# One kind of seven-product unit, with two weight sums kept in DRAM and two added where used: 66 units instead of 60

## The chip, the core and the metric

The kernel runs on one core of one Trainium2 chip. The core has a matrix engine (TensorE, PE in the profile; its weight loads are shown as PEld), a vector engine (VectorE, DVE), a scalar engine (ScalarE, ACT), a general engine (GpSimd, POOL) and a queue engine (SyncE, SP) that issues most of the transfers. TensorE writes into PSUM; the other operands live in SBUF, on 128 partitions, and the weights come from DRAM. The metric is the device time of one execution in microseconds (us); lower is better.

## The reference

A trunk of two pre-norm residual layers over 256 tokens of width 2048, in float32. Layer 0 mixes tokens by neighbourhood attention, layer 1 by a gated short convolution. After each comes a gated MLP of inner width 5632 with a depthwise convolution.

```python
def conv_glu_ffn(x, w_up, conv_w, conv_b, w_down):
    h = dwconv_centered(x @ w_up, conv_w) + conv_b
    g, u = jnp.split(h, 2, axis=-1)
    return (jax.nn.silu(g) * u) @ w_down

def reference(x, ...):
    h = x
    for i in range(DEPTH):
        a = rms_norm(h, mix_norm[i])
        ...
        h = h + mixed
        h = h + conv_glu_ffn(rms_norm(h, ffn_norm[i]), ...)
    return rms_norm(h, final_norm)
```

## The kernel before

**Precision.** Each float32 operand is split into a high part (a cast to the matmul type, ACT, L171 or L294) and a low part (what the cast left over, DVE, L172 or L295). A product is then three matmuls into one PSUM tile: high by high, high by low, low by high.

**Two kinds of stage.** A `Phase` computes one 128-column tile of a projection after another (query/key, up projection, short-conv input); its weight tile is the stationary operand, and its evacuations on ACT and DVE (convolution, gate, split into the next stage's activation tiles) lie beside the following matmuls. `Values` does the attention's values. A `Tokens` stage computes an output projection: `wo` after attention, two halves of the down projection in each layer (`down[layer, half]`, 22 tiles of input width each), and `wscout` after the short convolution (16 tiles). In a `Tokens` stage the activations are the stationary operand and the weights move, 512 columns at a time.

**Units.** A `Tokens` stage works on two groups `g` of 1024 output columns. In each it goes over pairs of input tiles; such a pair, with two halves of the tokens and two halves of the columns, is a unit: a two-by-two block product. A plain unit (P) does it with eight products, 24 matmuls. A seven-product unit does it with seven, 21 matmuls, after a scheme that needs four sums of blocks on either side. On the activation side these are the forms (`make_forms`, GpSimd and split, made in the stage before). On the weight side they are `t1` to `t4`, and there are two kinds of unit for them:

- S ("sums"): `left` and `right` blocks (512 KB each) are loaded, DVE adds all four sums where the unit is used (L180, L181, L183, L184, four adds of 128x512), and `w22`, `t1`/`t3` and `t4`/`t2` are split.
- D ("kept"): the four sums were made earlier and kept in DRAM. The unit loads `left` (512 KB), the block `w22` (256 KB, half a buffer) and two tiles of kept sums (512 KB each) and splits all four.

**Making sums ahead.** `make` (L189) handles half of a D unit: two loads of 256 KB into activation tiles that happen to be free (L199), four adds of 128x256 (L206 to L209) due four chunks later, two stores of 256 KB from ACT's queue (L214) due seven chunks later. `plan_jobs` lists these half jobs and `take` deals them out over the attention, up and short-conv stages that come before their use: `QK_JOBS`, `V_JOBS`, `UP_JOBS`, `SC_JOBS`.

**Order.** The plans (`S_FIRST`, `S_SECOND`, `S_OUT`, `S_ATT`) write out by hand, for each group, which unit is of which kind and in which order they run, and after how many items the combination of the unit's four extra PSUM tiles into `h` (`combine`, eight DVE operations) is due. There are 60 seven-product units: 12 in each of the four down projections, 8 in `wscout`, 4 in `wo`; 38 of them D and 22 S, of 120 units in all. What is loaded and split runs ahead of the matmuls by chunks (`prep_to`, `AHEAD` = 4): six `raw` buffers for what is loaded (`RAWS`), six each for high and low parts (`hi`, `lo`). A framework places the instructions on each engine's queue in an order of its own, close to that of the program; the engines then run in order.

**PSUM and SBUF.** The forms of the even tiles' three other blocks lie in six slots of the tags `sf`, `vv` and `qk`; the fourth goes over a quarter of the activation tile that no seven-product unit reads (`place`). There are 22 activation tiles.

Of the kernel before, what the change touches and what calls it, by code (L numbers as in the profile page):

```python
# [22 lines left out]
P = 128  # L23
# [22 lines left out]
def plan(text, due):  # L46


    words = text.split()
    return (tuple(int(x[1:]) for x in words), {int(x[1:]): x[0] for x in words if x[0] != "P"}, due)  # L50


S_FIRST = (plan("P0 D1 P2 S3 D4 P5 D6 S7 P8 D9 P10", 3), plan("P0 P2 D1 S3 D4 P5 D6 S7 P8 P10 D9", 6))
S_SECOND = (plan("P0 P2 D1 S3 D4 P5 D6 S7 D8 P9 P10", 1), plan("P0 P2 P5 D1 S3 D4 S7 D6 D8 P9 P10", 1))
S_OUT = (plan("P0 D1 S2 P3 D4 D5 P6 P7", 1), plan("P0 P3 D1 S2 D4 D5 P6 P7", 1))
QK_JOBS, V_JOBS, UP_JOBS, SC_JOBS = (0, 4, 4, 2), (2, 2, 2, 0), (10, 10, 12, 8), 20
S_ATT = (plan("P0 P1 P2 S6 P3 S7 P4 P5", 1),) * 2

# [19 lines left out]
def trunk(ctx, tc, xT, par, bias, wqk, wv, wo, wsc, wscout, wup, wdown, out):  # L78
# [49 lines left out]
    def prep_to(n):  # L128
        while len(prepped) < min(n, len(chunks)):
# [4 lines left out]
            if kind == "make":  # L134
                make(src, w)
                prepped.append(())
                continue
# [6 lines left out]
            if kind == "kept":  # L144
                newest["SP"] = nc.sync.dma_start(out=raw, in_=src().rearrange("p h n -> p (h n)"))
            else:
                newest["SP"] = nc.sync.dma_start(out=raw[:, :4 * w].rearrange("p (f c) -> p f c", f=4),
                                                 in_=src.rearrange("f p c -> p f c"))
            r = raw[:, :4 * w].rearrange("p (f k c) -> p f k c", f=4, c=P)
            if kind != "sums":  # L150
                prepped.append(parts(r) + (raw,))
            else:
                prepped.append(sums(prepped[-1][2].rearrange("p (f k c) -> p f k c", f=4, c=P), r))
# [21 lines left out]
    def sums(l, r):  # L175

        t13 = wp.tile([P, CH * P], F32, name="raw", tag="raw", bufs=RAWS)
        v13 = t13.rearrange("p (k f c) -> p f k c", f=4, c=P)
        add = nc.vector.tensor_add
        add(out=v13[:, :, 0, :], in0=l[:, :, 0, :], in1=r[:, :, 0, :])  # L180
        add(out=v13[:, :, 1, :], in0=r[:, :, 1, :], in1=r[:, :, 0, :])  # L181
        w22 = parts(r[:, :, 1:2, :])
        add(out=r[:, :, 1, :], in0=v13[:, :, 0, :], in1=r[:, :, 1, :])  # L183
        add(out=r[:, :, 0, :], in0=r[:, :, 1, :], in1=l[:, :, 1, :])  # L184
        return w22, parts(t13), parts(r)

    kept, newest = {}, {}

    def make(job, half):  # L189

        w, g, i = job
        if half == 0:
            kept[id(w), g, i] = dp.tile([P, 2, 2, 4 * P], F32, name=f"kept{len(kept)}")
        dst = kept[id(w), g, i]
        tiles = [act_tile().bitcast(F32) for _ in range(2)]
        for n, x in enumerate(tiles):
            f = 8 * g + 4 * n + 2 * half
            with tc.issue_after(newest["SP"].ins):
                nc.sync.dma_start(out=x.rearrange("p (f n) -> p f n", f=2),  # L199
                                  in_=w[f:f + 2, :, 2 * i * P:(2 * i + 2) * P].rearrange("f p n -> p f n"))  # L200
        l, r = (x.rearrange("p (f k c) -> p k f c", f=2, k=2) for x in tiles)

        def adds():
            add = nc.vector.tensor_add
            with tc.issue_after(newest["DVE"].ins):
                add(out=l[:, 0], in0=l[:, 0], in1=r[:, 0])  # L206
                add(out=r[:, 0], in0=r[:, 1], in1=r[:, 0])
                add(out=r[:, 1], in0=l[:, 0], in1=r[:, 1])
                add(out=l[:, 1], in0=r[:, 1], in1=l[:, 1])  # L209

        def store():
            for n, x in enumerate(tiles):
                with tc.issue_after(newest["ACT"].ins):
                    nc.scalar.dma_start(out=dst[:, n, half], in_=x)  # L214
        stores.append((len(prepped) + 4, adds))
        stores.append((len(prepped) + 7, store))
# [3 lines left out]
    def plan_jobs(w, plans):  # L220
        jobs.extend(((w, g, i), half) for g, (order, kinds, _) in enumerate(plans) for i in order if kinds.get(i) == "D"
                    for half in range(2))
# [5 lines left out]
    class Phase:  # L228
# [3 lines left out]
        def __init__(self, w, fts, nk, src, evac, intro=0, step=CH, jobs=()):  # L232
# [9 lines left out]
            for n, (two, ks) in enumerate(order):  # L242
# [5 lines left out]
                while made < min(len(jobs), max(0, -(-len(jobs) * (n + 1 - lo) // (hi - lo)))):  # L248
                    chunks.append((*jobs[made], "make"))
# [130 lines left out]
    class Tokens:  # L380
# [4 lines left out]
        def __init__(self, w, nk, src, evac, plan, forms, halves=0):  # L385
# [4 lines left out]
            for g, (order, kinds, _) in enumerate(plan):  # L390
                for i in order:
# [10 lines left out]
                    if kinds.get(i) == "S":  # L402
                        chunks.append((right, 2 * P, "sums"))
                        items.append((self, g, c + 1, k, k, k + 2))
                        ends.append(c + 2)
                    elif i in kinds:
                        chunks.append((right[:, :, P:], P, "cols"))
                        chunks.extend((lambda j=j, key=(id(w), g, i): kept[key][:, j], 2 * P, "kept") for j in range(2))
                        items.append((self, g, c + 1, k, k, k + 2))
                        ends.append(c + 4)  # L410
# [50 lines left out]
        def seven(self, g, c, k0):  # L461
# [8 lines left out]
            if sset[i] == "S":  # L470
                w22, (t1, t3), (t4, t2) = prepped[c][0], *([(y, j) for j in range(2)] for y in prepped[c][1:])
            else:
                w22, (t1, t4), (t3, t2) = prepped[c], *([(y, j) for j in range(2)] for y in prepped[c + 1:c + 3])
            s1, s2, s4, s3 = self.forms[i]
            raw = lambda k, t: tuple(self.src[k0 + k][:, j + t * P:j + (t + 1) * P] for j in (0, S))
            for ps, x, (w, j) in ((a, raw(0, 0), (left, 0)), ("11", raw(1, 0), (left, 1)), ("12", s4, (w22, 0)),
                                  (e, s1, t1), *((("21", raw(1, 1), t4),) * (sset[i] == "D")), (f, s3, t3), (b, s2, t2),
                                  *((("21", raw(1, 1), t4),) * (sset[i] == "S"))):
# [26 lines left out]
    form_at = [3]  # L505

    def make_forms(xe, xo, place):

        v = tp.tile([P, 4, P], F32, name="s", tag="s")
# [5 lines left out]
        if isinstance(place, tuple):  # L515
# [4 lines left out]
        n = form_at[0] = (form_at[0] + 1) % 6  # L520
        y = tp.tile([P, 6 * P], F32R, name="sf", tag=("sf", "vv", "qk")[n % 3])
        hi, lo = y[:, :3 * P], y[:, 3 * P:]
        split_into(hi, lo, v[:, :3].rearrange("p f c -> p (f c)"))
        spare = place[:, P:2 * P], place[:, 3 * P:]
        split_into(*spare, v[:, 3])
        return [(hi[:, j * P:(j + 1) * P], lo[:, j * P:(j + 1) * P]) for j in (0, 1)] + [
            spare, (hi[:, 2 * P:], lo[:, 2 * P:])]
# [116 lines left out]
    class Values:  # L644


        def __init__(self, g, src, jobs=()):
            self.g, self.src = g, src
            for k0 in range(0, KT, 2):
# [3 lines left out]
                if k0 in (4, 8)[:len(jobs)]:  # L653
                    chunks.append((*jobs[k0 // 8], "make"))
# [31 lines left out]
    def sc_evac(f, ps):  # L686
# [11 lines left out]
        else:  # L698
# [3 lines left out]
            if j % 2 == 0:  # L702
                sc_of["even"] = t
            elif j // 2 in S_OUT[0][1]:
                yforms[j // 2] = make_forms(sc_of["even"], t, yT[j - 1])
# [4 lines left out]
    def up_evac(layer, act, forms, sset):  # L710
        def evac(f, ps):
# [11 lines left out]
            else:  # L723
# [5 lines left out]
                elif j % HALF // 2 in sset:  # L729
                    forms[j % HALF // 2] = make_forms(glu["even"], c, act[j % HALF - 1])  # L730
# [247 lines left out]
```

## Time and profile before

| what | us |
|---|---|
| median of 3 runs | 2204.2 (2204.12 to 2206.07) |
| the profiled execution | 2203.89 |
| its span | 2202.1 |

The profile's page gives each engine's busy time with its share of the span and its number of instructions; then the span in 40 slices (PEclk is the TensorE clock that was granted, in tenths of full speed); then the chain of work that ended last, followed back from the last instruction. The views of the trace name a group or an instruction by its line in the kernel, its engine, its operation and its tiles (out <- in); a number in brackets behind an instruction of the timeline is how long the engine was idle before it, and who ended that. The matmuls are pipelined: the listed duration of one is longer than the step to the next.

| queue | packets | MB | share of 16 engines |
|---|---|---|---|
| SP's loads (q1) | 265360 | 488.07 | 68.3% |
| ACT's stores (q10) | 23264 | 40.49 | 4.9% |

### The profile page before, as it was taken

The page shows a single profiled execution, that of the slowest core. Times are in us where ns is not written, and L with a number is a line of the kernel's source. Part 1 is how long each engine was busy: PE and PEld are TensorE (multiplying, and loading weights), DVE is VectorE, ACT ScalarE, POOL GpSimd, SP SyncE. Part 2 cuts the span into 40 slices and gives each one's busy share as a digit, 9 for nine tenths or more (in the row PEclk, how much of TensorE's full clock was granted, in tenths as well). Part 3 has the DMA queues.
Part 4 walks back from the last instruction along what each step waited for, and adds up shares of the span by engine and source line. Part 5 has one row for each costly group of instructions (what it writes and reads, how often), then busy time and mean ns, then how long its engine had stood idle before and what let it go on. Part 6 is the DMA issues. An engine that isn't in the chain of part 4 may idle for free.

```text
span 2202.1 us, 33145 instructions
## 1 busy us (share of the span) xinstructions
PE 2184.6 (99%) x11728; PEld 1891.3 (86%) x11728; DVE 1835.8 (83%) x2960; ACT 1288.7 (59%) x1967; POOL 90.5 (4%) x143
## 2 busy tenths in 40 slices
PE   9999999999999999999999999999999999999997
PEld 8888888888888888888788888888888888888886
DVE  8788778888888788888897787898888887888888
ACT  7554556665655556566664445566656565666565
POOL 1001000000000000000000000000000000001000
PEclk9999999999999999999999999999999999999999
DMA  8787746777657777767798886787776786776585
GB/s 293 242 275 254 248 149 210 251 247 243 218 182 253 273 239 247 252 210 239 231 338 262 285 277 200 241 272 245 249 250 199 231 273 231 248 244 225 173 267 173
DMA packets 288790, 530.67 MB, mean 241 GB/s; under 512 B 19568, under 2 KB 187632, under 8 KB 288624
## 3 DMA queue, kind: packets, MB, share of 16 engines
q1 hardware_dynamic: 265360, 488.07, 68.3%
q10 hardware_dynamic: 23264, 40.49, 4.9%
q8 instruction: 92, 1.51, 0.3%
q14 instruction: 74, 0.61, 0.1%
HBM read 486.54 MB, written 41.94 MB: 240 GB/s over the span
## 4 chain that ended last, share of the span: by engine, by line
PE 88%; DVE 5%; DMA 5%; issue 1%; ACT 1%; SPq 0%; DVEq 0%; ACTq 0%
PE mm L262 40%; PE mm L270 21%; PE mm L458 6%; PE mm L459 6%; PE mm L457 6%; DMA act<-in_wdown 2%; DVE lo L172 2%; PE mu L458 2%; PE mu L459 2%; PE mu L457 2%; DMA raw<-in_wdown 1%; PE mm L665 1%; PE mm L667 1%; PE mm L666 1%; ACT hi L171 1%
## 5 line engine op out<-in xcount | busy, mean ns | idle before, releaser
L171 ACT CAST hi<-raw 128x1024 fp32r<-128x1024 f32 (+1 forms) x912 | 903.7, 1012 | 344.0 <-PE mm L459 91.7
L172 DVE TENSOR_TENSOR lo<-raw,hi 128x1024 fp32r<-128x1024 f32 (+1 forms) x852 | 1012.0, 1210 | 104.0 <-ACT hi L171 67.0
L262 PE MATMUL mm<-a,hi 128*128 128x512 f32 x4096 | 961.6, 391 | 0.5 <-DVE a L303 0.5
L262 PEld LDWEIGHTS mm<-a,hi 128*128 128x128 f32 x4096 | 759.2, 188 | 152.8 <-DVE a L303 1.6
L270 PEld LDWEIGHTS mm<-a,lo 128*128 128x128 f32 x4096 | 512.9, 191 | 14.3 <-DVE lo L172 2.4
L270 PE MATMUL mm<-a,lo 128*128 128x256 f32 x4096 | 518.6, 283 | 2.0 <-DVE lo L172 2.0
L457 PE MATMUL mm<-hi,act 128*128 128x512 f32 x656 | 255.7, 390 | 0.2 <-DVE h L350 0.2
L459 PE MATMUL mm<-hi,act 128*128 128x512 f32 x656 | 255.5, 390 | 0.0
L458 PE MATMUL mm<-lo,act 128*128 128x512 f32 x600 | 233.9, 390 | 0.6 <-DVE lo L172 0.5
L329 ACT ACTIVATE conv<-pad,pt 128x256 f32<-128x256 f32 x176 | 105.7, 601 | 205.6 <-DVE pad L321 203.8
L331 DVE SCALAR_TENSOR_TENSOR conv<-pad,pt,conv 128x256 f32<-128x256 f32 x384 | 183.8, 480 | 21.9 <-ACT conv L329 16.9
L315 ACT COPY corr<-mm 128x256 f32<-128x256 f32 x256 | 91.4, 370 | 163.1 <-PE mm L270 135.4
L457 PEld LDWEIGHTS mm<-hi,act 128*128 128x128 f32 x656 | 123.1, 188 | 25.9 <-issue 0.6
L459 PEld LDWEIGHTS mm<-hi,act 128*128 128x128 f32 x656 | 123.1, 188 | 25.4
L458 PEld LDWEIGHTS mm<-lo,act 128*128 128x128 f32 x600 | 112.7, 188 | 24.9 <-DVE lo L172 1.9
L316 DVE TENSOR_TENSOR corr<-mm,corr 128x256 f32<-128x256 f32 x256 | 106.7, 417 | 5.3 <-ACT corr L315 5.1
L206 DVE TENSOR_TENSOR act<-act 128x256 f32<-128x256 f32 x76 | 32.7, 431 | 75.7 <-DMA act<-in_wdown 59.6
L295 DVE TENSOR_TENSOR act<-conv,act 128x256 fp32r<-128x256 f32 x88 | 37.4, 425 | 60.6 <-ACT act L294 60.6
L321 DVE TENSOR_TENSOR pad<-corr,rstd 128x256 f32<-128x256 f32 x176 | 73.8, 419 | 0.2
L458 PE MATMUL mu<-lo,sf 128*128 128x512 f32 x168 | 65.9, 392 | 1.8 <-DVE lo L172 1.8
L459 PE MATMUL mu<-hi,sf 128*128 128x512 f32 x168 | 65.4, 389 | 0.0
L457 PE MATMUL mu<-hi,sf 128*128 128x512 f32 x168 | 65.4, 389 | 0.0
(158 smaller groups left out, 1540.3 us busy)
## 6 DMA issues: line engine op xcount, KB each, us to landing
raw<-in_wup SPq DMA_DIRECT2D x352, 512.0 KB, 5.2
raw<-in_wdown SPq DMA_DIRECT2D x144, 512.0 KB, 5.5
raw<-in_wsc SPq DMA_DIRECT2D x96, 512.0 KB, 5.6
kept<-act ACTq DMA_DIRECT2D x152, 256.0 KB, 4.1
raw<-kept SPq DMA_DIRECT2D x76, 512.0 KB, 4.9
act<-in_wdown SPq DMA_DIRECT2D x128, 256.0 KB, 5.9
raw<-in_wqk SPq DMA_DIRECT2D x56, 512.0 KB, 5.3
raw<-in_wv SPq DMA_DIRECT2D x32, 512.0 KB, 4.7
```

The costliest lines, as they stand in the source:

```text
L171: newest["ACT"] = nc.scalar.copy(out=hv, in_=r)
L172: newest["DVE"] = nc.vector.tensor_sub(out=lv, in0=r, in1=hv.bitcast(F32))
L262: nc.tensor.matmul(self.ps[ft], lhsT=prepped[i][0][:, o:o + P], rhs=self.src[k], start=k == 0, stop=False)
L270: nc.tensor.matmul(self.ps[ft][:, S:], lhsT=prepped[i][1][:, o:o + P], rhs=self.src[k][:, :S], start=False, stop=k == self.nk - 1)
L315: nc.scalar.copy(out=corr, in_=ps[:, S:])
L316: nc.vector.tensor_add(out=corr, in0=ps[:, :S], in1=corr)
L321: nc.vector.tensor_mul(out=dst, in0=both(ps), in1=rstd)
L329: nc.scalar.activation(c, x[:, 1:S + 1], AF.Identity, scale=w[1], bias=b)
L331: nc.vector.scalar_tensor_tensor(out=c, in0=x[:, tap:tap + S], scalar=w[tap], in1=c, op0=ALU.mult, op1=ALU.add)
L457: nc.tensor.matmul(ps, lhsT=xh, rhs=wh, start=start, stop=False)
L458: nc.tensor.matmul(ps, lhsT=xh, rhs=wl, start=False, stop=False)
L459: nc.tensor.matmul(ps, lhsT=xl, rhs=wh, start=False, stop=stop)
```

## The change

S and D units are replaced by one kind, H. Of the four weight sums `t1` and `t3` are kept in DRAM, as one tile of 512 KB, and `t2` and `t4` are added where the unit is used: `pair_of_sums` writes `t2 = t1 + w22` over the loaded `w22` in its own raw buffer, and `t4 = t2 +` a block of `left` into the half of that buffer that was empty; the buffer is then split as a whole. A job now handles a whole unit: three loads of 256 KB, two adds of 128x512, two stores of 256 KB.

```diff
+S_FIRST = (plan("P0 H1 H3 P2 H4 H5 P8 H6 H7 H9 P10", 3), plan("P0 P2 H1 H3 P8 H4 H5 H6 P10 H7 H9", 6))
+S_SECOND = plan("P0 P2 H1 H3 H4 P9 H5 H6 H7 H8 P10", 0)
+S_MLP = {(0, 0): S_FIRST, (0, 1): (S_SECOND, plan("P0 P2 P5 H1 H3 H4 P9 H6 H7 H8 P10", 0)),
+         (1, 0): S_FIRST, (1, 1): (plan("P0 P2 H1 H3 H4 P9 H6 H7 H8 P5 P10", 1), plan("P0 P2 H1 H3 P5 H4 H6 H7 P8 P9 P10", 0))}
+S_OUT = (plan("P0 H1 H2 P3 H4 H5 H7 P6", 0), plan("P0 P3 H1 H2 H4 H5 H7 P6", 0))
+S_ATT = (plan("P0 P1 P2 H6 P3 H7 P4 P5", 1),) * 2
+QK_JOBS, V_JOBS, UP_JOBS, SC_JOBS = (0, 4, 4, 0), (2, 3, 2, 0), (9, 8, 11, 8), 16
...
             if kind == "kept":
-                newest["SP"] = nc.sync.dma_start(out=raw, in_=src().rearrange("p h n -> p (h n)"))
...
+                newest["SP"] = nc.sync.dma_start(out=raw, in_=src())
+                t13 = parts(raw)
+                prepped.append((t13, parts(pair_of_sums(raw, prepped[-1][2], prepped[-2][2]))))
+                continue
...
+    def pair_of_sums(t13, w22, left):
+
+        l = left.rearrange("p (f k c) -> p k f c", f=4, c=P)
+        t2, t4 = w22[:, :4 * P], w22[:, 4 * P:].rearrange("p (f c) -> p f c", f=4)
+        nc.vector.tensor_add(out=t2, in0=t13[:, :4 * P], in1=t2)
+        nc.vector.tensor_add(out=t4, in0=t2.rearrange("p (f c) -> p f c", f=4), in1=l[:, 1])
+        return w22
...
-    def make(job, half):
...
+    def make(w, g, i):
+
+        kept[id(w), g, i] = dst = dp.tile([P, 8 * P], F32, name=f"kept{len(kept)}")
+        tiles = [act_tile().bitcast(F32) for _ in range(3)]
+        for x, f, k in zip(tiles, (0, 4, 4), (0, 0, 1)):
+            f, k = 8 * g + f, 2 * i + k
             with tc.issue_after(newest["SP"].ins):
...
+                nc.sync.dma_start(out=x.rearrange("p (f c) -> p f c", f=4),
+                                  in_=w[f:f + 4, :, k * P:(k + 1) * P].rearrange("f p c -> p f c"))
+        l, r, t = tiles
 
         def adds():
...
+                nc.vector.tensor_add(out=l, in0=l, in1=r)
+                nc.vector.tensor_add(out=t, in0=t, in1=r)
```

The units by stage become 4 in `wo`, 14 and 13 in layer 0's down projections, 10 in `wscout`, 14 and 11 in layer 1's. The two halves of the MLP now have plans for each layer (`S_MLP`), and the combination's due times change with them. In `seven` the product with `w22` and the four with sums keep their order, with the one that needs `t4` last. The forms follow: where a unit is of seven products in only one of the two groups, the fourth form can no longer lie over the activation tile, and gets a block of its own; a seventh form of a half is put into what the larger slots leave over.

```diff
+    form_at, left_over = [], []
+
+    def form_slots(blocks):
+
+        if not form_at:
+            return [left_over.pop() for _ in range(3)]
+        tag = next(x for x in form_at if blocks == 3 or x != "sf")
+        form_at.remove(tag)
+        y = tp.tile([P, (6 if tag == "sf" else 8) * P], F32R, name="sf", tag=tag)
+        if tag != "sf" and blocks == 3:
+            left_over.append(y[:, 6 * P:])
+        return y
```

The jobs of the value stage stand behind its second, fourth and sixth chunk instead of the third and fifth.

More of the change, by code (lines that the diff above doesn't have):

```diff
@@ L173, in split_parts @@
         return hi, lo
[L175 to L185, printed above, removed]
@@ L220, in plan_jobs @@
     def plan_jobs(w, plans):
-        jobs.extend(((w, g, i), half) for g, (order, kinds, _) in enumerate(plans) for i in order if kinds.get(i) == "D"
-                    for half in range(2))
+        jobs.extend((w, g, i) for g, (order, sset, _) in enumerate(plans) for i in order if i in sset)
     def take(n):
@@ L704, in sc_evac, with up_evac @@
             elif j // 2 in S_OUT[0][1]:
-                yforms[j // 2] = make_forms(sc_of["even"], t, yT[j - 1])
+                yforms[j // 2] = make_forms(sc_of["even"], t, in_both(S_OUT, j // 2) and yT[j - 1], not yforms)
     glu = {}
-    def up_evac(layer, act, forms, sset):
+    def up_evac(layer, act, forms, plans):
         def evac(f, ps):
```

116 lines of the change are left out of this document (47 added, 69 removed).

## The prediction

> **What bounds the kernel now.** I read the page first, its busy shares and the chain that ended last, then TensorE's own waits, the windows of the stretches in which two-by-two units run, and in these the VectorE's timeline.
>
> ```profile
> PE 2184.6 (99%) x11728; PEld 1891.3 (86%) x11728; DVE 1835.8 (83%) x2960; ACT 1288.7 (59%) x1967; POOL 90.5 (4%) x143
> PEclk9999999999999999999999999999999999999999
> PE 88%; DVE 5%; DMA 5%; issue 1%; ACT 1%; SPq 0%; DVEq 0%; ACTq 0%
> ...
> PE bc L781 <- DVE conv L779: 3.7, 2, 3.2
> PE mm L270 <- DVE lo L172: 2.0, 2, 1.1
> PE mu L458 <- DVE lo L172: 1.8, 4, 0.7
> PE st L111 <- DVE inv L740: 1.1, 1, 1.1
> ...
> PE mm L458 <- DVE lo L172: 0.5, 1, 0.5
> ```
>
> TensorE is at work in 99% of the span, at full granted clock, and 88% of the chain is its own matmuls. Its waits are small: 3.7 us belong to the closing norm, and what is left for faster feeding is 2.0 + 1.8 + 0.5 = 4.3 us, all of it waits for VectorE's low part of a weight block (L172). So a matmul less is time less, as long as VectorE keeps pace; VectorE, at 83%, is the engine that could stop it. By stretch, the columns being us, busy PE, PEld, DVE, ACT, POOL, clock, DMA share, GB/s:
>
> ```profile
> 306.00:394.00 88.00, 88.00 (x408) 73.36 (x408) 71.67 (x90) 51.36 (x72) 4.84 (x8) 1.00 0.60 196
> 641.84:753.39 111.55, 111.55 (x495) 92.35 (x493) 92.52 (x107) 66.91 (x74) 0.00 (x0) 1.00 0.77 251
> 997.85:1108.90 111.05, 109.78 (x489) 89.56 (x488) 96.88 (x116) 69.75 (x88) 0.00 (x0) 1.00 0.75 250
> 1113.86:1385.10 271.24, 269.25 (x1553) 238.07 (x1552) 211.24 (x375) 137.51 (x201) 9.61 (x16) 1.00 0.81 264
> 1385.10:1468.00 82.90, 82.90 (x376) 68.67 (x375) 73.63 (x91) 52.08 (x67) 0.00 (x0) 1.00 0.79 261
> 1716.90:1828.44 111.54, 111.54 (x494) 92.35 (x493) 92.42 (x107) 67.10 (x74) 0.00 (x0) 1.00 0.77 251
> 2072.91:2190.00 117.09, 115.79 (x522) 94.72 (x520) 98.86 (x125) 70.10 (x92) 0.00 (x0) 1.00 0.66 217
> ```
>
> In order: `wo`; first and second down projection of layer 0; the short-conv input projection; its output projection; first and second down projection of layer 1, the last with part of the end. TensorE fills all but 1.3 us of each down projection and all of the output projection.
>
> **What the change removes: 18 matmuls.** A plain unit (P) issues 8 products of 3 matmuls, a seven-product unit 21. The first down projection of layer 0 has 12 seven-product and 10 plain units, 12 x 21 + 10 x 24 = 492 matmuls in 111.55 us: 0.227 us each. (A matmul's listed duration, 390 ns, is its latency; they overlap.) Six more units make 6 x 3 x 0.227 = 4.08 us less on the engine that sets the end. By the plans: +2 in each first down projection, +1 and -1 in the second ones, +2 in the output projection, none in `wo`.
>
> **VectorE's price of a unit**, by starts in its timeline of the first down projection:
>
> ```profile
> 698.65 2.35 DVE L172 TENSOR_TENSOR lo<-raw,hi 128x1024 fp32r<-128x1024 f32 x2
> 700.91 0.68 DVE L499 TENSOR_TENSOR h<-h,mu 128x512 f32<-128x512 f32 x1
> ...
> 703.92 0.68 DVE L172 TENSOR_TENSOR hi<-raw,hi 128x512 fp32r<-128x512 f32 x1
> 704.52 2.35 DVE L172 TENSOR_TENSOR lo<-raw,hi 128x1024 fp32r<-128x1024 f32 x2
> ```
>
> Two low parts of 1024 take 2.26 us from start to start, 1.13 each; the five adds of 512 from 700.91 to 703.92 take 0.60 each, and so does a low part of 512. Hence P: 2 x 1.13 = 2.26. A D unit (sums all kept in DRAM): 3 x 1.13 + 0.60 = 3.99. An S unit (all sums made where used): 3.99 + 4 x 0.60 = 6.39. The new H unit, with two adds where used: 3.99 + 1.20 = 5.19. TensorE gives a seven-product unit 21 x 0.227 = 4.77 us and a P unit 5.45. So D ran ahead of TensorE, H falls 0.4 us behind it each time, and only P units win that back. By stretch:
> - first down projections: 8 D + 4 S + 10 P = 80.1 becomes 14 H + 8 P = 90.7. VectorE 92.5 + 10.7 = 103.2 us in 111.55 - 1.36 = 110.2: 94%.
> - second, layer 0: 13 H + 9 P = 87.8, +7.7: 104.6 of 110.4, 95%.
> - output projection: 6 D + 2 S + 8 P = 54.8 becomes 10 H + 6 P = 65.5. 73.6 + 10.7 = 84.3 of 81.5 us: 103%.
> - second, layer 1: 11 H + 11 P = 82.0, +1.9: 100.8 of 117.8, 86%, and its last unit goes.
> - `wo`: 4 S become 4 H, -4.8 us: no risk.
>
> The output projection's excess must come from the lead with which VectorE enters:
>
> ```profile
> 1383.37 0.69 DVE L181 TENSOR_TENSOR raw<-raw 128x512 f32<-128x512 f32 x1
> ...
> 1385.36 0.40 PE L457 MATMUL mm<-hi,act 128*128 128x512 f32 x1
> ```
>
> When TensorE starts on unit 0, VectorE has for 2 us been at the sums of unit 2, which TensorE needs 5.45 + 4.77 us later: a lead of some 10 us.
>
> **The wait that H adds.** ACT may cut the second pair of sums into its high part only after the second add, and VectorE then waits for ACT. The S unit has the same chain, and its cost is to be seen (VectorE, ACT, TensorE):
>
> ```profile
> 1087.89 0.68 DVE L184 TENSOR_TENSOR raw<-raw 128x512 f32<-128x512 f32 x1
> 1089.77 2.36 DVE L172 TENSOR_TENSOR lo<-raw,hi 128x1024 fp32r<-128x1024 f32 x2 [1.19 <-ACT hi L171]
> ...
> 1088.69 4.49 ACT L171 CAST hi<-raw 128x1024 fp32r<-128x1024 f32 x5 [2.01 <-DVE raw L184]
> ...
> 1091.05 0.50 PE L458 MATMUL mu<-lo,sf 128*128 128x512 f32 x1 [0.75 <-DVE lo L172]
> ...
> 676.16 0.69 DVE L184 TENSOR_TENSOR raw<-raw 128x512 f32<-128x512 f32 x1
> 676.77 5.91 DVE L172 TENSOR_TENSOR lo<-raw,hi 128x1024 fp32r<-128x1024 f32 x5
> ```
>
> At 1087.89 the last sum leaves VectorE idle for 1.19 us and TensorE for 0.75; at 676.16 another low part was ready and it cost nothing. Queued behind a waiting low part are VectorE's later low parts and the combine, and TensorE waits for these. So H's wait lies between 0 and 1.19 us; I take 0.6, the middle, as both rows are of the same operation. Then the demand is 103.2 + 14 x 0.6 = 111.6 of 110.2 in the first down projections, 104.6 + 7.8 = 112.4 of 110.4 in the second of layer 0, 84.3 + 6.0 = 90.3 of 81.5 in the output projection: short by 1.4, 2.0 and 8.8 us, each under the lead of 10. The last leaves 1.2 us, and late in a run of H units the lead is no longer whole. I put 2.0 us of new TensorE waits there (bounds 0 and 5).
>
> **Sums, loads and stores ahead.** 76 half jobs of four adds of 256 become 66 jobs of two of 512.
>
> ```profile
> 1267.02 0.43 DVE L206 TENSOR_TENSOR act<-act 128x256 f32<-128x256 f32 x1 [3.90 <-DMA act<-in_wdown]
> ...
> 1269.84 0.42 DVE L209 TENSOR_TENSOR act<-act 128x256 f32<-128x256 f32 x1
> 1270.17 0.42 DVE L206 TENSOR_TENSOR act<-act 128x256 f32<-128x256 f32 x1
> ...
> 1271.78 0.62 PE L270 MATMUL mm<-a,lo 128*128 128x256 f32 x3 [0.86 <-DVE lo L172]
> ...
> raw<-in_wdown SPq DMA_DIRECT2D x144, 512.0 KB, 5.5
> kept<-act ACTq DMA_DIRECT2D x152, 256.0 KB, 4.1
> raw<-kept SPq DMA_DIRECT2D x76, 512.0 KB, 4.9
> ...
> raw<-in_wdown SPq DMA_DIRECT2D x32, 256.0 KB, 3.9
> ```
>
> By starts an add of 256 is 0.33 us, so 76 x 4 x 0.33 = 100 us become 66 x 2 x 0.60 = 79. These lie beside the up and short-conv projections, where TensorE sets the pace, and are worth nothing by themselves; they can ease the 0.86 us and its like. Stores fall from 152 to 132 on ACT's queue. SP issues 3 loads a job instead of 2 a half job, 198 for 152, and one read back a unit for two. Bytes of a unit: 1 MB of job traffic each way and 1.75 MB at use for D; for H 0.75 in, 0.5 out, 1.25 at use. S and P units have no job and draw 1 MB. In all 38 x 3.75 + 22 + 6 = 170.5 MB become 66 x 2.5 = 165, so I cost transfers at nothing, hidden by the matmuls.
>
> The raw buffers are the cover that could go: H holds `left`, `w22` and `kept`, half of six, until its last add, so the next loads start late; a landing of 3.9 to 5.5 us against 4.77 us a unit just fits. It is in the 2.0 us.
>
> **The sum.** The profiled run took 2203.89 us (span 2202.1), 0.3 under the median 2204.2; removal and waits are differences, so I count from the median: 2204.2 - 4.08 + 2.0 = 2202.1. In the second down projection of layer 1 one unit goes and three P units stand between its last H unit and the end, so its waits can go:
>
> ```profile
> 2165.42 0.50 PE L458 MATMUL mu<-lo,sf 128*128 128x512 f32 x1 [0.57 <-DVE lo L172]
> 2174.15 0.50 PE L458 MATMUL mu<-lo,sf 128*128 128x512 f32 x1 [0.23 <-DVE lo L172]
> 2180.05 0.50 PE L458 MATMUL mm<-lo,act 128*128 128x512 f32 x1 [0.49 <-DVE lo L172]
> ```
>
> 0.57 + 0.23 + 0.49 = 1.29 us less: **2200.8 us**. What is late next there is the closing norm, unchanged.
>
> **The rivals.**
> 1. *The feeding gets better, not worse* (the wait is filled, as at 676.16, and the 4.3 us of waits go): 2204.2 - 4.08 - 4.3 = 2195.8, and half of it 2198. For it: S units, at 6.39 us the dearest, are gone and the adds in the short-conv stretch are a fifth fewer. Against it: 94 to 103% in four stretches.
> 2. *VectorE becomes the bound* (slower). Its place is the runs of three to five H units, its price the full 1.19 us at each: 119.9 of 110.2, 120.1 of 110.4, 96.2 of 81.5 and 119.8 of 110.2, over by 9.7, 9.7, 14.7 and 9.6. With a lead of 7.5 us in each (the 10 is seen at one entry only) 2.2 + 2.2 + 7.2 + 2.1 = 13.7 us are left: 2204.2 - 4.08 + 13.7 - 1.29 = 2212.5. With the whole lead it is 4.7 us, without any 43.7. It decides from about 0.7 us a unit, where the output projection's lead is spent. For it: 1087.89. Against it: 676.16.
> 3. *The jobs' loads come late.* An add waited 3.90 us for its load of 256 KB tiles, and H's job loads three tiles where a half job loaded two; by 5.5 against 3.9 us, 256 KB more is 1.6 us. Two such waits cost TensorE 2.0 us together; with five of 1.0 + 1.6 it is 13 us instead, 11 more, and 2200.8 + 11 = 2211.8; with three, 5.8 more, 2206.6. For it: the jobs' loads come in runs of 128 x 4 = 512 B instead of 1 KB. Against it: loads in such runs (`w22`, 256 KB) land in 3.9 us, stores of the same size in longer runs in 4.1, and there are fewer jobs. The Trainium skill (Perfetto Trace Analysis, DMA Optimizations) holds that transfers in pieces under 2 KB carry a marked overhead each. By that rule this rival would be the likeliest, at 2211.8 against the sum's 2200.8; the trace, with 3.9 beside 4.1 us, does not bear it out.
>
> That the units would not be made can't be: the plans fix the matmuls.
>
> **Chances.** Forecast (2199 to 2203) 0.46; rival 1 0.27; rival 2 0.17; rival 3 0.10. A measurement of this kernel tells about 0.2% (4.4 us) from no change: the bounds are 2199.8 and 2208.6. Faster: rival 1 and a little of the forecast, 0.33. Slower: most of rival 2 and some of rival 3, 0.17. Same 0.50. The range runs from rival 1 with nearly all its waits gone, 2196, to 2209.5, which leaves out the dearer part of rivals 2 and 3.
>
> **What would show it.** TensorE with 11710 matmuls, its busy time about 4 us lower. VectorE's busy time nearly unchanged in total (+37 at the units, -21 at the jobs), but at 93% or more in the first down projections. Right: TensorE's waits for L172 at 3 to 6 us, near the end of the output projection. Rival 1: under 2 us. Rival 2: over 10, with low parts waiting for ACT after the second add. Rival 3: the same waits, but in the up and short-conv stretches behind adds that wait for a load. Wrong altogether: a matmul step other than 0.227 us.

## The result, and the profile after

The changed kernel took **2219.9 us** (median; 2217.6 to 2223.5) where the kernel before took 2204.2 beside it: ratio **1.0071** [1.0053, 1.0088], slower by 15.7 us. The forecast was 2200.8 us in a range of 2196.0 to 2209.5. In another set of runs the same kernel gave 1.0063 [1.0049, 1.0076]. Some later runs stood beside a kernel before of 2207.1 us, so experiments are compared by ratio.

The page of the changed kernel, its busy shares and its chain:

```profile
PE 2190.1 (99%) x11710; PEld 1887.3 (85%) x11710; DVE 1853.0 (84%) x2856; ACT 1290.4 (58%) x1991; POOL 109.0 (5%) x159
PE 73%; DVE 15%; issue 5%; ACT 3%; DMA 3%; SPq 0%; POOL 0%; ACTq 0%; DVEq 0%
```

TensorE has its 18 matmuls fewer, yet its busy time rose by 5.5 us, 9.6 above what fewer matmuls give (5.5 + 4.1), and its share of the chain fell from 88% to 73%; VectorE's rose from 5% to 15%. The 99% hides this: of the 9.6 us, 3.4 are two stretches in which the clock was at half (last section), and the rest are stalls too short to stand as a gap between two pipelined matmuls, so that they count as busy. What TensorE lost is read from the length of the stretches. These are the windows of the four stretches with more units (first down projection and second of layer 0, output projection, first down projection of layer 1; us, then busy PE, PEld, DVE, ACT, POOL, clock, DMA share, GB/s), each from the stretch's first matmul to the next stage's. Here is after:

```profile
640.91:754.48 113.57, 112.24 (x490) 91.12 (x489) 101.50 (x119) 65.80 (x76) 0.00 (x0) 1.00 0.70 227
998.49:1118.13 119.64, 115.10 (x507) 92.69 (x506) 107.46 (x131) 71.63 (x91) 0.00 (x0) 1.00 0.69 216
1391.99:1483.45 91.46, 86.10 (x373) 68.59 (x372) 82.44 (x106) 54.49 (x73) 2.36 (x3) 0.98 0.65 208
1730.22:1847.27 117.05, 113.44 (x491) 90.78 (x490) 105.20 (x124) 66.13 (x79) 0.00 (x0) 1.00 0.69 219
```

and here the same whole stretches of the kernel before where the prediction's windows were cut otherwise:

```profile
997.85:1113.86 116.01, 114.74 (x511) 93.66 (x509) 101.84 (x123) 72.03 (x90) 0.00 (x0) 1.00 0.76 254
1385.36:1468.98 83.62, 83.62 (x379) 69.20 (x377) 74.35 (x92) 52.82 (x70) 0.00 (x0) 1.00 0.80 263
```

In the first and the last of the four windows after, two matmuls of the up projection stand among the last ones; their 0.45 us are taken off below. With the matmuls that went (0.227 us each) taken from the length before, the new stall is:

| stretch | before | less matmuls | after | new stall | forecast shortage | waits of some 1.19 us for ACT after the second add |
|---|---|---|---|---|---|---|
| first down proj., layer 0 | 111.55 | 110.19 | 113.12 | 2.93 | 1.4 | 8 of 14 units |
| second down proj., layer 0 | 116.01 | 115.33 | 119.64 | 4.31 | 2.0 | 8 of 13 |
| output projection | 83.62 | 82.26 | 91.46 | 9.20 | 8.8 | 5 of 10 |
| first down proj., layer 1 | 111.54 | 110.18 | 116.60 | 6.42 | 1.4 | 8 of 14 |

That is 22.9 us. Not all of it is the order: 1.7 us in the output projection are a stretch at half clock (last section), and some 1.5 of the last row stand at that stretch's entry, behind an evacuation on VectorE. The short-conv stretch is 2.4 us longer (below), 4.1 us of matmuls went, and the rest, with the second down projection of layer 1, is some 4 us shorter: +17.0 us of span, 2219.1 against 2202.1. What an H unit costs is seen best late in the output projection, in its run of five. VectorE's timeline (start, us, engine, line, operation; the last bracket is the idle time before it):

```profile
1454.02 2.36 DVE L180 TENSOR_TENSOR lo<-raw,hi 128x1024 fp32r<-128x1024 f32 x2 [1.17 <-ACT hi L179]
1456.29 0.69 DVE L180 TENSOR_TENSOR hi<-raw,hi 128x512 fp32r<-128x512 f32 x1
1456.90 1.22 DVE L180 TENSOR_TENSOR lo<-raw,hi 128x1024 fp32r<-128x1024 f32 x1
1458.03 0.69 DVE L159 TENSOR_TENSOR raw<-raw 128x512 f32<-128x512 f32 x1
1458.75 0.69 DVE L160 TENSOR_TENSOR raw<-raw 128x512 f32<-128x512 f32 x1
1460.63 2.36 DVE L180 TENSOR_TENSOR lo<-raw,hi 128x1024 fp32r<-128x1024 f32 x2 [1.19 <-ACT hi L179]
...
1467.24 2.36 DVE L180 TENSOR_TENSOR lo<-raw,hi 128x1024 fp32r<-128x1024 f32 x2 [1.19 <-ACT hi L179]
```

ACT's in the same place, and what TensorE's matmuls on the last of these units wait for:

```profile
1459.55 3.47 ACT L179 CAST hi<-raw 128x1024 fp32r<-128x1024 f32 x4 [3.15 <-DVE raw L160]
```

```profile
1474.33 0.50 PE L442 MATMUL mu<-hi,sf 128*128 128x512 f32 x1 [1.51 <-ACT hi L179]
```

One unit takes VectorE 6.61 us (1460.63 to 1467.24) against TensorE's 4.77. VectorE makes the low part of the first pair of sums (L180 at 1456.90), then the two adds, and then has nothing it may do: the low part of the second pair needs ACT's high part, and ACT starts that when the second add lands. ACT had stood idle for 3.15 us till then. The two engines wait for each other in turn, and TensorE for both. In TensorE's waits the line has changed: in the units it is mostly ACT's high part (L179), 7.9 + 2.0 us, which the forecast's signs did not look for. VectorE's low part (L172 before, L180 now) is late there by 1.1 us only; the 2.2 us below are in the short-conv stretch. The low parts' 3.3 us together would by their size have passed for the forecast's own sign of being right, 3 to 6 us (us in total, times, longest):

```profile
PE mu L442 <- ACT hi L179: 7.9, 12, 1.5
PE mm L259 <- DVE lo L180: 2.2, 1, 2.2
PE mm L442 <- ACT hi L179: 2.0, 7, 0.7
PE mu L443 <- DVE lo L180: 1.1, 2, 0.6
```

### The profile page after: what moved, and what is told of

It is laid out like the page before. It is cut to its first block, busy times and chain, and to the rows that moved or that the text cites. A ratio compares the mean times of both kernels' runs of the same rounds, so it can differ in the third digit from the quotient of the medians.

```text
span 2219.1 us, 33057 instructions
## 1 busy us (share of the span) xinstructions
PE 2190.1 (99%) x11710; PEld 1887.3 (85%) x11710; DVE 1853.0 (84%) x2856; ACT 1290.4 (58%) x1991; POOL 109.0 (5%) x159
## 3 DMA queue, kind: packets, MB, share of 16 engines
q8 instruction: 92, 1.51, 0.3%
## 4 chain that ended last, share of the span: by engine, by line
PE 73%; DVE 15%; issue 5%; ACT 3%; DMA 3%; SPq 0%; POOL 0%; ACTq 0%; DVEq 0%
PE mm L251 36%; PE mm L259 19%; DVE lo L180 7%; PE mm L444 3%; PE mm L443 3%; PE mm L442 3%; ACT hi L179 3%; DVE raw L160 1%; PE mm L668 1%; PE mm L670 1%; PE mm L669 1%; DVE raw L159 1%; DVE hi L180 1%; DMA act<-in_wdown 1%; DMA raw<-in_wup 1%
## 5 line engine op out<-in xcount | busy, mean ns | idle before, releaser
L180 DVE TENSOR_TENSOR lo<-raw,hi 128x1024 fp32r<-128x1024 f32 (+1 forms) x858 | 1020.3, 1214 | 121.4 <-ACT hi L179 70.7
L179 ACT CAST hi<-raw 128x1024 fp32r<-128x1024 f32 (+1 forms) x924 | 905.1, 1009 | 371.7 <-DVE raw L160 136.2
L442 PE MATMUL mm<-hi,act 128*128 128x512 f32 x624 | 245.0, 394 | 5.3 <-DVE h L339 2.1
L444 PE MATMUL mm<-hi,act 128*128 128x512 f32 x624 | 243.8, 391 | 0.0
L443 PE MATMUL mm<-lo,act 128*128 128x512 f32 x564 | 220.5, 391 | 0.0
L320 DVE SCALAR_TENSOR_TENSOR conv<-pad,pt,conv 128x256 f32<-128x256 f32 x384 | 178.3, 480 | 27.3 <-ACT conv L318 20.7
L442 PEld LDWEIGHTS mm<-hi,act 128*128 128x128 f32 x624 | 117.6, 188 | 33.2 <-ACT hi L179 5.0
L444 PEld LDWEIGHTS mm<-hi,act 128*128 128x128 f32 x624 | 117.4, 188 | 24.3
L443 PEld LDWEIGHTS mm<-lo,act 128*128 128x128 f32 x564 | 106.4, 189 | 22.1
L305 DVE TENSOR_TENSOR corr<-mm,corr 128x256 f32<-128x256 f32 x256 | 104.7, 417 | 10.4 <-ACT corr L304 10.2
L198 DVE TENSOR_TENSOR act<-act 128x512 f32<-128x512 f32 x66 | 45.9, 695 | 67.2 <-DMA act<-in_wdown 45.2
L442 PE MATMUL mu<-hi,sf 128*128 128x512 f32 x186 | 73.5, 395 | 7.3 <-ACT hi L179 7.3
L443 PE MATMUL mu<-lo,sf 128*128 128x512 f32 x186 | 73.4, 395 | 1.1 <-DVE lo L180 1.1
L444 PE MATMUL mu<-hi,sf 128*128 128x512 f32 x186 | 72.5, 390 | 0.0
```

The source lines that it names most:

```text
L179: newest["ACT"] = nc.scalar.copy(out=hv, in_=r)
L180: newest["DVE"] = nc.vector.tensor_sub(out=lv, in0=r, in1=hv.bitcast(F32))
L305: nc.vector.tensor_add(out=corr, in0=ps[:, :S], in1=corr)
L320: nc.vector.scalar_tensor_tensor(out=c, in0=x[:, tap:tap + S], scalar=w[tap], in1=c, op0=ALU.mult, op1=ALU.add)
L442: nc.tensor.matmul(ps, lhsT=xh, rhs=wh, start=start, stop=False)
L443: nc.tensor.matmul(ps, lhsT=xh, rhs=wl, start=False, stop=False)
```

## The experiments

In the expectations, W is the theory that the 1.19 us wait behind the second add is what costs, V that VectorE's work alone is too much, and B that the raw buffers are held too long.

**e1: the two adds ahead of the low part that they do not need.** In the branch for kept sums; `pair_of_sums` also returns its second add. The low part of the first pair is then work for VectorE while ACT casts the second.

```diff
-                t13 = parts(raw)
-                prepped.append((t13, parts(pair_of_sums(raw, prepped[-1][2], prepped[-2][2]))))
+                hi, lo = (wp.tile([P, CH * P], F32R, name=n, tag=n, bufs=6) for n in ("hi", "lo"))
+                newest["ACT"] = nc.scalar.copy(out=hi, in_=raw)
+                t24, added = pair_of_sums(raw, prepped[-1][2], prepped[-2][2])
+                with tc.issue_after(added.ins):
+                    newest["DVE"] = nc.vector.tensor_sub(out=lo, in0=raw, in1=hi.bitcast(F32))
+                prepped.append(((hi, lo), parts(t24)))
```

> The two adds of an H unit are put ahead of the low part of t1/t3 on VectorE, so that this low part (1.13 us) fills the time in which ACT makes the high part of t2/t4. Same work, same loads. Theory W (the forced wait of 1.19 us after the second add, in 38 of 66 units, is what slows the changed kernel): no such waits, the output projection of layer 1 goes from 91.5 us to 84 to 87, the time to 2203 (2200 to 2208). Rival V (VectorE's work alone is too much in the runs of H units, 5.4 us a unit against 4.77): waits go, time stays near 2215. Rival B (raw buffers held too long, loads late): the order of the adds is nothing to it, 2217 to 2223.

Measured: 0.9977 [0.9968, 0.9986] of the kernel before; run again in another set, 0.9975 [0.9966, 0.9984]. VectorE's timeline in the same run of units:

```profile
1446.50 1.22 DVE L151 TENSOR_TENSOR lo<-raw,hi 128x1024 fp32r<-128x1024 f32 x1
1447.79 2.36 DVE L184 TENSOR_TENSOR lo<-raw,hi 128x1024 fp32r<-128x1024 f32 x2
1450.07 0.68 DVE L184 TENSOR_TENSOR hi<-raw,hi 128x512 fp32r<-128x512 f32 x1
1450.78 0.69 DVE L163 TENSOR_TENSOR raw<-raw 128x512 f32<-128x512 f32 x1
1451.51 0.69 DVE L164 TENSOR_TENSOR raw<-raw 128x512 f32<-128x512 f32 x1
1452.12 1.22 DVE L151 TENSOR_TENSOR lo<-raw,hi 128x1024 fp32r<-128x1024 f32 x1
1453.39 2.36 DVE L184 TENSOR_TENSOR lo<-raw,hi 128x1024 fp32r<-128x1024 f32 x2
```

and its windows of the output projection and the first down projection:

```profile
1383.85:1467.76 83.91, 83.05 (x373) 67.69 (x371) 81.58 (x104) 54.51 (x73) 2.36 (x3) 1.00 0.70 221
640.88:751.07 110.19, 110.19 (x489) 91.22 (x487) 103.38 (x120) 68.46 (x77) 0.00 (x0) 1.00 0.74 234
```

A unit now takes 5.62 us (1446.50 to 1452.12), 1.0 less than 6.61, from the same instructions: the low part at L151 fills the wait. The output projection falls from 91.5 to 83.9 us from its first matmul to the next stretch's, the first down projection to the 110.19 that its matmuls need, the second of layer 0 to 113.9; the first of layer 1 takes 112.2 in this profile and 110.2 in the second. The median is 2202.4 us beside a kernel before of 2207.2, W's 2203; what V and B expect, 2215 and 2217 to 2223, did not come. Units, tiles and transfers are those of the changed kernel, so its whole loss was the order of two adds and one low part. By ratio e1 stands at 2199.1 us, where the forecast's sum without any new wait gives 2198.8 (2204.2 - 4.08 - 1.29). That is in part luck: the short-conv stretch of e1 is 2.9 us longer than before, and the second down projection of layer 0 is 1.5 us shorter than its matmuls account for.

**e3: the wait in more units.** The adds are held behind the low part of the first pair in each unit, which in the changed kernel was left open and came about in 37 of 66.

```diff
                 t13 = parts(raw)
-                prepped.append((t13, parts(pair_of_sums(raw, prepped[-1][2], prepped[-2][2]))))
+                with tc.issue_after(newest["DVE"].ins):
+                    t24 = pair_of_sums(raw, prepped[-1][2], prepped[-2][2])
+                prepped.append((t13, parts(t24)))
```

> The opposite of the first: the adds are put behind the low part of t1/t3 in all 66 units, so that nearly all of them have the wait (some are filled by other work). Same work, same loads. W: up to 28 waits more of 1.19 us, most of them felt in the runs of H units: 2235 (2228 to 2250). V and B: within 3 us of the changed kernel's 2219.9.

Measured: 1.0171 [1.0156, 1.0186], median 2244.4 us. 50 of the 66 units waited for ACT, 60.2 us in all. TensorE's waits of e3, where L444 is the first matmul of a product:

```profile
PE mu L444 <- ACT hi L181: 16.9, 23, 1.5
PE mm L261 <- DVE lo L182: 4.1, 3, 1.8
```

13 more waits than in the changed kernel, 16.1 us more of them (60.2 less 44.1), and 25 us more of span (2244.1 against 2219.1). By ratio the time is 2241.9 us beside 2204.2: within W's 2228 to 2250, above its middle, and far from V and B. As many as 28 more waits were expected, and 13 did this; the 9 us of span beyond the waits themselves were not followed.

**e2: the output projection with the 8 units of the kernel before**, all else as changed:

```diff
-S_OUT = (plan("P0 H1 H2 P3 H4 H5 H7 P6", 0), plan("P0 P3 H1 H2 H4 H5 H7 P6", 0))
+S_OUT = (plan("P0 H1 H2 P3 H4 H5 P6 P7", 1), plan("P0 P3 H1 H2 H4 H5 P6 P7", 1))
```

> The output projection of layer 1 alone goes from 5 + 5 H units back to 4 + 4, with two P units at the end of each group; 6 more matmuls (1.4 us). If the loss there comes from the density of H units (W and V), that stretch falls from 91.5 us to 84 to 86 and the time to 2213 (2211 to 2215). If it were lost elsewhere and only shows there, the time stays at 2220 or a little above.

Measured: 1.0029 [1.0019, 1.0038], and 84.1 us in the output projection instead of 91.5. The median is 2212.5 us, by ratio 2210.6: at the 2211 to 2215 expected if the density of H units is what costs. Two units less bring 7.3 us there although they cost 1.4 us of matmuls; 1.7 of the 7.3 are the stretch at half clock, which this profile does not have there. Runs of three and five H units have become runs of two and four, and these the lead covers to within 0.5 us (84.13 against 83.62 before).

**e5: 60 H units, at the places and due times of the 60 before.**

```diff
-S_FIRST = (plan("P0 H1 H3 P2 H4 H5 P8 H6 H7 H9 P10", 3), plan("P0 P2 H1 H3 P8 H4 H5 H6 P10 H7 H9", 6))
...
+S_FIRST = (plan("P0 H1 P2 H3 H4 P5 H6 H7 P8 H9 P10", 3), plan("P0 P2 H1 H3 H4 P5 H6 H7 P8 P10 H9", 6))
+S_SECOND = (plan("P0 P2 H1 H3 H4 P5 H6 H7 H8 P9 P10", 1), plan("P0 P2 P5 H1 H3 H4 H7 H6 H8 P9 P10", 1))
+S_MLP = {(layer, half): (S_SECOND if half else S_FIRST) for layer in range(2) for half in range(2)}
+S_OUT = (plan("P0 H1 H2 P3 H4 H5 P6 P7", 1), plan("P0 P3 H1 H2 H4 H5 P6 P7", 1))
```

> H units, but only 60 of them, in the places, orders and due times of the kernel before; 18 matmuls more than the changed kernel (4.1 us). Parts the kind of unit from their number. W: the waits stay in runs of two, a P unit behind each: 2208 (2205 to 2214). V: VectorE needs 6 us more than before in each down projection and stays under TensorE's time: 2204 to 2206. B: as slow as the changed kernel, 2215 to 2223, since each H unit holds its buffers as long.

Measured: 1.0049 [1.0033, 1.0065], median 2217.25 us, by ratio 2215.0: just outside W's range and at the lower edge of B's, the highest of the three. 36 of its 60 units waited, 42.1 us. Its first down projections lost only 1.4 us each against the kernel before, with 9 of 12 units waiting, their H units standing singly, in twos and once in three; its second ones, with runs of three and of six, lost 4.8 and 3.5 us, the short-conv stretch 4.0. So the number of waits alone does not give the time: how many units follow one another matters too, and those places had been laid out for units of another price. Of the 4.8 and the 4.0 us, 1.7 each are a stretch at half clock (from 1105.13 and 1245.08). Ahead of the second of these TensorE stood for 2.40 us (until 1244.64), after a sum made ahead had waited 3.67 us for its load (1238.48). This run misses W as I had sized it; e1, with more units and no waits, still shows what removes the loss, and speaks against B, since its units hold as many buffers.

**e4: the order of e1 in the kernel before**, whose S units have the same two last adds; and **e0**, the changed kernel beside it.

```diff
+        hi, lo = (wp.tile([P, CH * P], F32R, name=n, tag=n, bufs=6) for n in ("hi", "lo"))
+        newest["ACT"] = nc.scalar.copy(out=hi, in_=t13)
         add(out=r[:, :, 1, :], in0=v13[:, :, 0, :], in1=r[:, :, 1, :])
-        add(out=r[:, :, 0, :], in0=r[:, :, 1, :], in1=l[:, :, 1, :])
-        return w22, parts(t13), parts(r)
+        added = add(out=r[:, :, 0, :], in0=r[:, :, 1, :], in1=l[:, :, 1, :])
+        with tc.issue_after(added.ins):
+            newest["DVE"] = nc.vector.tensor_sub(out=lo, in0=t13, in1=hi.bitcast(F32))
+        return w22, (hi, lo), parts(r)
```

> The kernel before with the order of e1 in its 22 S units: the low part of the first pair of sums is put behind the last add. Theory W (what costs is the 1.19 us wait of VectorE after the last add, in whatever unit): before had 6 such waits, 7.2 us, in 22 units, and TensorE lost 4.3 us to low parts, so 2 to 4 us go: ratio 0.998 to 0.999, and the second down projection of layer 0 falls from 116.0 to some 114. Rival (the order helps for another reason, in proportion to units): a third of what e1 gained on the changed kernel, 6 us, ratio 0.997. Beside e1 it tells what the change is worth once no unit waits: 18 matmuls, 4.1 us, if VectorE keeps pace in both.

> The changed kernel itself beside the others on one chip: ratio 1.007 to the kernel before, and 1.009 to 1.010 to e1 if both ratios hold on another chip.

Measured: e4 0.9986 [0.9977, 0.9995], e0 1.0063 as told, which is 1.0086 of e1 by the ratios, a little under the 1.009 expected. All waits after the last add are gone in e4, but its profile shows no gain: span 2203.0 us against 2202.1, the second down projection of layer 0 115.9 against 116.0, where some 114 was expected. The 0.75 us that TensorE stood at 1091.05 before are gone, but 0.40 and 0.28 us stand a few units later. What is late ahead of the first of these is shown by ACT, VectorE and TensorE in e4:

```profile
1097.98 1.05 ACT L171 CAST hi<-raw 128x1024 fp32r<-128x1024 f32 x1 [1.16 <-DMA raw<-kept]
1099.06 1.23 DVE L172 TENSOR_TENSOR lo<-raw,hi 128x1024 fp32r<-128x1024 f32 x1 [0.90 <-ACT hi L171]
1100.35 0.50 PE L462 MATMUL mu<-lo,sf 128*128 128x512 f32 x1 [0.40 <-DVE lo L172]
```

The high part waits 1.16 us for the load of a tile of kept sums, the low part for the high part, and TensorE for the low part: with the order's wait gone, this comes last. Why the load is late was not followed. Each kernel has one profile here, so the 0.9 us of span tells little. Order was worth some 19 us to a kernel of 66 H units and at most 5 us (by the interval) to one of 22 S units. Between e1 and e4 stands what the change is worth once neither waits: 0.9975 to 0.9986, with intervals that overlap, so 4.1 us is neither shown nor excluded.

**e6, e7 and e9: what is left of rival 3**, on top of e1. e6 makes the sums two chunks later, e7 moves seven jobs out of the short-conv stretch, e9 does both.

```diff
-        stores.append((len(prepped) + 4, adds))
+        stores.append((len(prepped) + 6, adds))
...
-        stores.append((len(prepped) + 7, store))
+        stores.append((len(prepped) + 9, store))
```

```diff
-QK_JOBS, V_JOBS, UP_JOBS, SC_JOBS = (0, 4, 4, 0), (2, 3, 2, 0), (9, 8, 11, 8), 16
+QK_JOBS, V_JOBS, UP_JOBS, SC_JOBS = (0, 4, 4, 0), (2, 3, 2, 0), (12, 12, 11, 8), 9
```

> e1 with the sums made ahead two chunks later (6 instead of 4 chunks behind their loads' issue, stores 9 instead of 7). What is left of rival 3: in the short-conv stretch of e1 TensorE is idle for 3.6 us behind sums that wait for their loads. If that is so, the idle time there falls under 2 us and the kernel is 2 to 3 us faster than e1, 2199 to 2200 at e1's 2202.4 (ratio to before 0.9965). If those stalls come from the order of VectorE's other work, the time stays within 1 us of e1.

> e1 with 9 instead of 16 jobs in the short-conv stretch, the others in the up projections of layer 0 (12 and 12 instead of 9 and 8), where VectorE has more idle time. If the stalls left in the short-conv stretch (3.6 us idle in e1) come from low parts queued behind sums that wait for their loads, they fall to 1 to 2 us and the kernel is 2 to 3 us faster than e1 (ratio 0.9985 to 0.999 of e1); if the load of transfers or the order there is what stalls, the time stays or the stalls turn up in the up projections.

> e7 with the sums two chunks later, as in e6: at best all of the 3.6 us go, ratio 0.998 of e1; if neither decides, within 1 us of e1.

> e1 beside them on the same chip: ratio to the kernel before 0.9975 to 0.998, 0.991 of the changed kernel.

The reason for them is in the short-conv stretch of the changed kernel, VectorE and TensorE:

```profile
1272.10 0.69 DVE L198 TENSOR_TENSOR act<-act 128x512 f32<-128x512 f32 x1 [4.10 <-DMA act<-in_wdown]
...
1276.99 1.21 DVE L180 TENSOR_TENSOR lo<-raw,hi 128x1024 fp32r<-128x1024 f32 x1
```

```profile
1278.26 2.01 PE L259 MATMUL mm<-a,lo 128*128 128x256 f32 x8 [2.17 <-DVE lo L180]
```

A sum made ahead waits 4.10 us for its load, the low parts behind it on VectorE are late, and TensorE stands for 2.17 us: rival 3 as it was written, at one place in this profile. The kernel before had two shorter stalls in the same stretch, 0.9 us (1271.78) and 1.1 us (1306.51).

Measured: e6 0.9973 [0.9962, 0.9984], e7 0.9971 [0.9961, 0.9982], e9 0.9983 [0.9975, 0.9992], beside e1's 0.9975. By these intervals none is told from e1, and the 2 to 3 us that e6 and e7 were expected to gain if rival 3 was left in them are not shown. In e6 TensorE is idle for 2.9 us of the short-conv stretch (3.6 in e1 when first run, 4.4 when run again): two chunks do not help. In e7 it is 0.7 us, and that stretch takes 270.5 us instead of 274.4 and 276.6; but the second down projection of layer 0 takes 117.4 instead of 113.9, and the up projection ahead of it 1.0 more. With e9 these two take 118.1 and 250.3 (244.5 in e1). Jobs that were moved did stall their new neighbours: in e7 a job's add waits 2.57 us for its load (938.45) and TensorE then 0.74 us (940.29), in e9 2.64 us (919.09) and 1.61 us (923.09), both in the up projection. But the longest new stall, 2.74 us at 1001.62 in e7 and 2.38 at 1006.25 in e9, stands at the entry of the second down projection behind an evacuation on VectorE; in e7 no job's add lies in the 60 us before it, and e1 does not have it. What causes it was not followed, so it is not shown that moving the jobs merely moves the stall. Single profiles also differ by the stretches at half clock, 1.7 us each: there is one in the short-conv stretch of e6 and of e1's second profile, and one in the second down projection of e9. e1, e6, e7 and e9 are all faster than both kernels.

## Why the prediction was wrong

- **The 18 matmuls** are gone and are worth their 4.08 us: the first down projection of e1 takes 110.19 us, 1.36 less than before, to the hundredth.
- **VectorE's price of an H unit** was 5.19 us; without its wait it is 5.42 (6.61 less 1.19), and in e1, where nothing waits, such a unit takes 5.62. The second add reads the first one's result, and its start came 0.72 us after the first's, with another 0.69 until ACT may begin: 1.41 us for the two, where 2 x 0.60 from independent adds was put. Over 14 units that is 3 us more demand (6 by e1's price), left out of the sum. VectorE's busy time in total rose by 17.2 us, as forecast (37 - 21 = 16); its share in the first down projections was 90%, not 93% or more, since waiting does not count as busy.
- **The wait of 0.6 us a unit** was about right: 37 of 66 units waited some 1.19 us, 44.1 us or 0.67 a unit.
- **The failing step is the lead: "short by 1.4, 2.0 and 8.8 us, each under the lead of 10".** The forecast saw the shortage and set a lead of 10 us against it, so that 2.0 us of stalls were left. The runs show 22.9 us. A lead near 10 us was there at the entry of the four stretches (10.2, 8.0, 10.2 and 10.1 us before), and at the entry only: in the output projection the trace of before already shows it mostly spent a dozen microseconds later, as VectorE did the last work of the short-conv projection. VectorE and TensorE of the kernel before, at unit 2 of the output projection and again near its end:

```profile
1394.28 5.91 DVE L172 TENSOR_TENSOR lo<-raw,hi 128x1024 fp32r<-128x1024 f32 x5
1397.85 0.39 PE L458 MATMUL mu<-lo,sf 128*128 128x512 f32 x1
...
1453.05 5.21 DVE L172 TENSOR_TENSOR lo<-raw,hi 128x1024 fp32r<-128x1024 f32 x4 [2.00 <-ACT hi L171]
1455.61 0.39 PE L458 MATMUL mu<-lo,sf 128*128 128x512 f32 x1
```

The first low part of each row is made in 1.22 us and ends at 1395.50 and 1454.27; TensorE uses it 2.35 and 1.34 us later. Each low part's end paired with the first matmul that uses it, the smallest lead of the kernel before was 1.4 us in the first down projection, 1.6 in that of layer 1, 1.3 in the output projection and 0.05 in the second of layer 0. That, and not 10, was what the stretches could give. Each H unit with its wait takes 1.84 us of it (6.61 less 4.77), so a run of three takes 5.5 and one of five 9.2. As an estimate: with no lead at all, the forecast's own shortages are 1.4 + 2.0 + 8.8 + 1.4 = 13.6 us, and with 0.23 us more for each of the 51 units (5.42 less 5.19) 25.3, against the 22.9 measured.
- **A demand of 94% of a stretch** was read as safe. It is a mean over plain and H units, and the lead that plain units win is not kept: in the changed kernel, first group of the output projection, it fell from 7.2 us or more at unit 1 to 1.5 in unit 2, and came back to 9.2 at the plain unit that opens the second group, only to be 0.1 at that group's last H unit.
- **The 2.0 us of new waits** thus came out more than ten times too small (22.9), and their upper bound of 5 was passed as well.
- **The 1.29 us that go in the second down projection of layer 1** are there in size, but only in part at the place named: from that stretch's start to the end it is 127.9 us instead of 129.2. Its last matmul comes 117.01 us after its first, 117.04 before, and it has one seven-product unit less (+0.68), so some 0.7 us of its waits went. The other 1.3 us went in the closing norm behind it (12.15 to 10.85 us), which the forecast called unchanged. The size is right partly by luck.
- **The jobs at nothing** held for the time of their adds. The short-conv stretch is 2.4 us longer, of which 1.7 are a stretch at half clock behind the stall of 2.17 us; the jobs' loads landed in a median of 6.2 us, where the half jobs' took 5.9.
- **The rivals.** Rival 2 was right in its mechanism and its place, not in its terms: it needed all units to wait and allowed 7.5 us of lead; 37 waited, and the lead was a few microseconds or none. "From about 0.7 us a unit" is near the 0.67 measured, but with the true lead it would have decided far below. Its chance of 0.17 rested on one such wait (1087.89) against one that cost nothing (676.16). What told them apart was which low part VectorE had at hand, a thing of order, and e1 shows that this order could be had.

## What to carry to other kernels

Where one engine feeds another in a stretch that is nearly full, read the lead of the feeder at its tightest place along the stretch, not at the entry, and set the shortage of each run of dear units against that, not the mean of the stretch. A step that hands over to a second engine and back needs independent work behind the hand-over, and the order that gives it has to be pinned where the feeder has a choice. When the bounding engine is 99% busy both before and after, compare stretch lengths: stalls of pipelined matmuls are counted as busy.

## What the hardware showed unexpectedly

A stall can cost more than its length. In these windows of the changed kernel the granted TensorE clock is the figure behind the five busy times:

```profile
1274.95:1278.36 3.41, 1.24 (x11) 1.04 (x9) 3.41 (x7) 2.45 (x3) 0.00 (x0) 1.00 0.90 256
1278.36:1281.77 3.41, 3.41 (x13) 3.02 (x14) 3.38 (x6) 1.44 (x2) 0.00 (x0) 0.50 1.01 244
1281.77:1285.18 3.41, 3.41 (x16) 2.83 (x15) 2.23 (x2) 0.80 (x1) 0.00 (x0) 1.00 0.85 306
1472.92:1476.33 3.41, 1.78 (x6) 1.13 (x7) 2.84 (x4) 3.09 (x4) 0.00 (x0) 1.00 0.81 264
1476.33:1479.74 3.41, 3.41 (x9) 2.65 (x9) 3.41 (x4) 2.69 (x3) 0.00 (x0) 0.50 0.75 193
```

After the stall of 2.17 us that ends at 1278.26 the clock was at half for 3.41 us, and again after that of 1.51 us at 1474.33; half of 3.41 us, 1.7, is lost each time, which is most of what the short-conv stretch lost. The kernel before has no such window ahead of its last microseconds, although it has a stall of 1.1 us.

The length of the stall does not decide. e7 kept the full clock through its stall of 2.74 us, which lies across two such windows:

```profile
996.59:1000.00 3.41, 2.29 (x11) 1.54 (x9) 2.22 (x5) 3.31 (x7) 0.00 (x0) 1.00 0.45 143
1000.00:1003.41 3.41, 1.66 (x6) 1.05 (x6) 3.41 (x7) 0.34 (x1) 0.00 (x0) 1.00 0.24 70
```

e6 lost it after stalls of 1.06 and 0.85 us that lie within one. In the clock records of the twelve profiles, the falls of one profile lie whole multiples of 3.413 us apart. On that grid each of the 11 falls ahead of the closing norm stands at the end of a window in which TensorE was busy for 30 to 53%, and behind the first microseconds no window above 53% has one; but three windows of 49 to 53% (in e7, e0 and e9) have none, so the edge is not sharp in these figures. e1 kept its clock at 1270 in a window that was 66% busy; when it was run again, the stall there was 2.3 us, the window 39% busy, and the clock fell. The Trainium skill (TensorE: Matmul & The Clock Gate, Part 1) has the clock fall to half after an idle window of some 3.4 us. The length of the slow window agrees with it; here a window that was idle for about half was enough.
